# Layer 1's routing without GpSimd, its gather ahead of the overflow's loop, and that loop in a conditional with a branch hint for TensorE

## Chip, cores and metric

One core of one Trainium2 chip runs the whole program in one launch. The metric is device time in microseconds, the median of several executions. All data is float32 in HBM; the 475 MB that the kernel moves are nearly all expert weights.

## What is computed

The reference is a transformer of two layers on 512 tokens of width 1024, conditioned by a vector `c`. Layer 0 mixes tokens by attention, layer 1 by pooling; in each a mixture of 32 experts follows. Cut to what matters here:

```python
for i in range(2):
    sh_m, sc_m, g_m, sh_f, sc_f, g_f = split(silu(c) @ w_ada[i] + b_ada[i], 6)
    x = x + g_m * mixer[i](modulate(rms_norm(x, norm_mix_g[i]), sh_m, sc_m))    # attention, then pooling
    tokens = modulate(rms_norm(x, norm_ffn_g[i]), sh_f, sc_f)
    x = x + g_f * hierarchical_moe(tokens, w_rg[i], w_re[i], w_gu[i], w_down[i])
return rms_norm(x, final_norm_g)

def hierarchical_moe(h, w_rg, w_re, w_gu, w_down):
    gate_g, grp = top_k(softmax(h @ w_rg), 1)              # one of 4 groups
    le = (h @ w_re).reshape(T, 4, 8)[arange(T), grp]       # its 8 experts
    top_v, top_i = top_k(le, 2)                            # the best two
    w_sel = gate_g * softmax(top_v)
    # every token goes to its two experts: (silu(h @ gate) * (h @ up)) @ down, summed with weights w_sel
```

## The kernel before

Instructions stand on each engine in the order in which the code issues them. SyncE's queue streams the weights (class `Stream`, line 118) into a ring of 1 MB tiles; a transfer is issued when a tile comes free, which TensorE's use of an earlier one decides, and `st.fill(n)` says how many may be under way ahead of use.

The stages are: attention (0 to 325 us), its out-projection with layer 0's routing interleaved (`norm_attended`, to 370), the MoE of layer 0 (to 843), the pooling layer with layer 1's routing at its end (`pool_layer` and `route`, to 909), the MoE of layer 1 (to 1387) and the final norm.

Routing of a layer, whose names occur below:

- `norm_high` (L1160, ScalarE) writes a token tile times its norm, rounded, to `xnp`; a second `xnp` holds the low remainder. Layer 0 makes it with `norm_low` (L1164, VectorE, in two halves). Layer 1 goes through `split_norm`: ScalarE makes the same product once more in full (`y`, L1175), and GpSimd subtracts (L1176). There are four token tiles of 128 tokens (`NT`).
- `logits` on TensorE, then `add_shift` (L1186), `choose` (L1222 to L1240: the maxima and their one-hots `r_og`, `r_oh`, then the table `r_M` of tokens and experts), all VectorE.
- `rank` (TensorE L1249, VectorE `r_rk` L1253) counts a token's place within its expert; `fullest_of` (L1260, L1261) counts the fullest expert's tokens, `spread_two` writes `r_oh` for all 32 experts.
- `one_hot` (L1541, VectorE) turns `r_rk` into `OH`, by which TensorE gathers the tokens of a group of four experts (L1014 in layer 0, L1338 elsewhere, 64 matmuls); ScalarE (L1350) and VectorE (L1348) modulate the result to `xe`, in eight tiles.

Each expert has room for `CAP` = 64 tokens. `overflow` stands ahead of each MoE: it copies `r_rk` to `r_tmp` (L1491), every engine loads the fullest expert's count (L1492), and a loop `For_i(CAP, n, CAP)` (L1493) runs the 16 pairs of experts once more for what is over. With these inputs no expert is over 64, so the loop's body is skipped; its code stands between the branch and what follows. In the built program the skip is a compare that falls through, an unconditional branch to the loop's exit, and there a string of semaphore instructions by which all engines wait for each other.

In layer 0 the first group is gathered and modulated ahead of the loop; `moe` gets it as `first`. In layer 1 it is gathered behind it, in `moe`. Then come 16 pairs of experts: `pgate` and `pup` (L1361), `py` (L1386), `pc` (L1415). In the first pair, after 24 of its matmuls, TensorE has the products `pw` (L1321) that sort the tokens' shares into slots; they need `r_rhs` (L1318), the end of VectorE's chain that begins with the one-hots of group 1 and goes over the shares (L1281 to L1297) and `ro` (L1315).

Of the kernel before, what the change touches and what calls it, by code (L numbers as in the profile page):

```python
# [11 lines left out]
F32 = mybir.dt.float32  # L12
F32R = mybir.dt.float32r
# [137 lines left out]
def in_two(z):  # L151

    return z.rearrange("p (q k s) -> p q k s", s=128, k=2)
# [25 lines left out]
class Kernel:  # L179
# [3 lines left out]
    def build(self):  # L183
        tc, nc, a = self.tc, self.nc, self.a
        with ExitStack() as es:
# [12 lines left out]
            with ExitStack() as sm:  # L198
# [7 lines left out]
                norms = self.moe(0, self.prepare_pool(), first=xe, later=later)  # L206
                if self.stop == "moe0":
                    return self.dump_x()
                self.pool_layer(norms)
                if self.stop == "pool":  # L210
                    return self.dump_x()
                self.route()
                self.final(self.moe(1, self.prepare_final(), self.gained))
# [753 lines left out]
    def norm_attended(self):  # L967
# [33 lines left out]
        banks, hl = {}, {}  # L1001
        low = lambda j, k: self.norm_low(j, r[j], *hl[j], k)

        def zeros(k, tag):
            banks[k] = pm.tile([128, 512], F32, tag=tag, name="pga")
            nc.tensor.matmul(banks[k], self.tri_b[:, 0:1].to_broadcast([128, 128]), self.ones_b[:, 0:1].to_broadcast([128, 512]),
                             start=True, stop=False)

        def gather(k, js, parts=range(2)):

            for z in range(2):
                for j in js:
                    for part in parts:
                        nc.tensor.matmul(banks[k][:, z * 256:(z + 1) * 256],  # L1014
                                         self.parts[part][j // 2][:, j % 2, (k + z) * 128:(k + z + 1) * 128], OH[:, j], start=False,
                                         stop=(z == 1 and j == NT - 1 and part == 1))
# [64 lines left out]
        xe = self.big([128, KD, 256], F32, "xe")  # L1081
        for k in range(0, KD, 2):
            gather(k, range(3, 4), (0,))
        for k in range(0, KD, 2):
            gather(k, range(3, 4), (1,))
            for z in range(2):
                self.modulated(0, k + z, banks[k][:, z * 256:(z + 1) * 256], xe[:, k + z])
# [78 lines left out]

    def split_norm(self, j, r, y=None):

        nc = self.nc
        hi, lo = self.norm_high(j, r)  # L1170
        if y is None:
            for k in range(2):
                self.norm_low(j, r, hi, lo, k)
        else:
            nc.scalar.activation(in_two(y), by_two(self.x(j)), AF.Copy, scale=r)  # L1175
            nc.gpsimd.tensor_tensor(lo, y, hi.bitcast(F32), op=ALU.subtract)  # L1176
# [90 lines left out]
    def route(self):  # L1267

        self.route_begin()
        self.choose(slice(0, NT))  # L1270
        self.rank(range(NT))
        self.fullest_of()
        self.spread_two()

# [56 lines left out]
    def gather(self, i, k, OH, n, xe):  # L1331
# [9 lines left out]
        self.modulated(i, k, p[:, :n], xe)  # L1341

# [141 lines left out]
    def overflow(self, i, gf):  # L1484
# [8 lines left out]
        with tc.For_i(CAP, n, CAP):  # L1493
            nc.vector.tensor_scalar(rko, rko, -float(CAP), None, op0=ALU.add)

            whl = self.shares()
            with tc.For_i(0, NPAIR, 1) as p:
                rp = mp.tile([128, NT, 2], F32, name="rp")
                nc.vector.tensor_copy(rp, rko[:, :, ds(2 * p, 2)])
                wp = mp.tile([128, NT, 8], F32R, name="wp")  # L1500
                tw = mp.tile([128, 2, NT, 2], F32, name="tw")
                for z in range(2):
                    for c in range(2):
                        nc.vector.tensor_tensor(tw[:, c], self.oh[c][:, :, ds(2 * p, 2)],
                                                whl[:, z, c].bitcast(F32)[:, :, None].to_broadcast([128, NT, 2]), op=ALU.mult)
                    nc.vector.tensor_tensor(wp[:, :, 2 * z:2 * z + 2], tw[:, 0], tw[:, 1], op=ALU.add)
                nc.vector.tensor_copy(wp[:, :, 4:8], self.tcol[:, :, None].to_broadcast([128, NT, 4]))
                OH = mp.tile([128, NT, 128], F32R, tag="scat", name="OHo", bufs=2)
                for j in range(NT):
                    nc.vector.tensor_tensor(OH[:, j].rearrange("p (e s) -> p e s", e=2),  # L1510
                                            self.iota[:, None, 0:CAP].to_broadcast([128, 2, CAP]),
                                            rp[:, j, :, None].to_broadcast([128, 2, CAP]), op=ALU.is_equal)
                pw = pm.tile([128, 512], F32, tag="t", name="pwo")
                for j in range(NT):
                    nc.tensor.matmul(pw[:, 0:8], OH[:, j], wp[:, j], start=(j == 0), stop=(j == NT - 1))
                s = mp.tile([128, 8], F32, name="so")
                nc.vector.tensor_copy(s, pw[:, 0:8])
                w = mp.tile([128, 1], F32, name="wo")
                for e in range(2):
                    q = slice(64 * e, 64 * e + 64)  # L1520
                    nc.vector.tensor_tensor(w[q], s[q, e:e + 1], s[q, 2 + e:3 + e], op=ALU.add)

                xe = self.fw[:, 1].rearrange("p (k n) -> p k n", k=KD)
                for k in range(KD):
                    self.gather(i, k, OH, 128, xe[:, k])

                def load(name, k):
                    q = slice(k // 2 * 256, (k // 2 + 1) * 256)
                    nc.sync.dma_start(wts, a[name][i, ds(2 * p, 2), q].rearrange("e (p k) n -> p e k n", k=2)[:, :, k % 2])
                    return wts[:, 0], wts[:, 1]  # L1530

                act = self.up(lambda k: xe[:, k], 0, lambda k: load("moe_w_gate_up", k))
                y = self.down(self.turn_act(act), lambda k: load("moe_w_down", k), w, gf)
                P = self.scatter(s[:, 4:5])
                for h in range(2):
                    for unit in self.combine(P, y[h], h):
                        unit()
# [13 lines left out]
    def moe(self, i, late, then=lambda: None, first=None, later=iter(())):  # L1551
# [3 lines left out]
        xe, OH = ({0: first}, {}) if first is not None else ({}, {0: self.one_hot(0)})  # L1555
# [35 lines left out]
        for k in range(KD if first is None else 0):  # L1591
            gather(0, k)
# [61 lines left out]
    def pool_layer(self, norms):  # L1654
# [138 lines left out]
        y = []  # L1793
# [12 lines left out]
        st.fill(RING + 1)  # L1806
        for j in range(1, NT):
            parted(j)
        self.fw = self.gw
        self.row_bcast(self.bank, 5, self.fw[:, 0], nc.scalar)  # L1810

    def row_load(self, name, rows):
# [62 lines left out]
```

## Time and profile before

| | us |
|---|---|
| median of 3 runs | 1399.34 (1399.21 to 1399.42) |
| the profiled execution's own time | 1400.81 |
| its span from first to last instruction | 1398.9 |
| TensorE busy | 1315.8 (94%) |
| VectorE busy | 672.5 (48%) |
| ScalarE busy | 367.7 (26%) |
| GpSimd busy | 153.2 (11%) |
| mean granted TensorE clock | 0.979 of full speed |

All times of rows are microseconds from the span's start in the profiled execution. A busy share is a mean over stages of different kinds; the stages around the change have their own rows below. Branches, semaphore and register instructions are not counted as busy; they are listed on the sequencers (PEldq is TensorE's).

### The profile page before, as it was taken

Reading aid. Unit: us, or ns where it says so; the run is one execution under the profiler, and the core shown is the slowest. Engines: PE = TensorE matmul, PEld = TensorE weight load, DVE = VectorE, ACT = ScalarE, POOL = GpSimd, SP = SyncE. Lnnn points to the kernel's source line nnn. Section 1 sums busy time; section 2 is a strip of 40 time slices with the busy share of each in tenths; the row PEclk is TensorE's granted clock in tenths of the full one; section 3 lists DMA queues with packets and bytes.
Section 4 is the critical chain, followed back from the end, with each engine's and each line's share of the span. In section 5 each row is a group of like instructions: output and inputs, shape, how many; then the busy total and the mean of one; then the engine's idle time right before and its main releaser. Section 6 shows DMA issues by size and latency. Waiting matters only on the chain. (4 is left out here: it accounts for less than half of the span.)

```text
span 1398.9 us, 18564 instructions
## 1 busy us (share of the span) xinstructions
PE 1315.8 (94%) x7134; PEld 737.9 (53%) x7135; DVE 672.5 (48%) x1288; ACT 367.7 (26%) x707; POOL 153.2 (11%) x142
## 2 busy tenths in 40 slices
PE   3799999999899999999999997689999999999995
PEld 1588677778545444454445444554445544454432
DVE  2777788768714343342433437633333433343325
ACT  2454678753211111111111114521111111111103
POOL 1523254430000000000000104200000000000001
PEclk9899999999999999999999998889999999999998
DMA  9412845179489999999999999259999999999993
GB/s 379 155 61 69 353 155 178 52 249 353 182 350 427 426 427 426 427 427 426 427 427 427 420 419 417 98 236 375 426 427 427 426 426 426 427 426 427 426 420 146
DMA packets 80558, 475.45 MB, mean 340 GB/s; under 512 B 8496, under 2 KB 10048, under 8 KB 30288
## 3 DMA queue, kind: packets, MB, share of 16 engines
q1 hardware_dynamic: 80456, 474.19, 82.7%
q8 instruction: 59, 0.97, 0.3%
q14 instruction: 35, 0.29, 0.1%
q10 hardware_dynamic: 8, 0.01, 0.0%
HBM read 472.06 MB, written 2.11 MB: 339 GB/s over the span
## 5 line engine op out<-in xcount | busy, mean ns | idle before, releaser
L1361 PE MATMUL pgate<-wt,xe 128*64 128x512 f32 x1024 | 266.3, 596 | 4.8 <-issue 4.8
L1361 PE MATMUL pup<-wt,xe 128*64 128x512 f32 x1024 | 265.4, 595 | 0.0
L1386 PE MATMUL py<-wt,aT 128*64 128x512 f32 x960 | 212.6, 595 | 0.0
L1366 DVE TENSOR_TENSOR act<-act,pup 128x512 f32<-128x512 f32 x32 | 22.0, 687 | 336.5 <-ACT act L1365 307.0
L1417 DVE TENSOR_TENSOR x<-x,pc 128x512 f32<-128x512 f32 x240 | 153.9, 683 | 32.3 <-PE pc L1415 32.3
L1361 PEld LDWEIGHTS pgate<-wt,xe 128*64 128x64 f32 x1024 | 74.3, 138 | 148.1 <-issue 138.1
L1361 PEld LDWEIGHTS pup<-wt,xe 128*64 128x64 f32 x1024 | 75.0, 138 | 146.5 <-issue 146.4
L1338 PE MATMUL pga<-OH,xnp 128*128 128x256 f32 x960 | 135.2, 286 | 5.5 <-issue 5.5
L1415 PE MATMUL pc<-y,scat 128*128 128x512 f32 x480 | 136.3, 405 | 2.5 <-DVE x L1417 2.5
L1338 PEld LDWEIGHTS pga<-OH,xnp 128*128 128x128 f32 x960 | 128.0, 190 | 14.2 <-issue 7.3
L1399 DVE SCALAR_TENSOR_TENSOR py<-py,r_sw,gw 128x512 f32<-128x512 f32 x64 | 48.5, 758 | 177.5 <-PE py L1386 168.5
L1386 PEld LDWEIGHTS py<-wt,aT 128*64 128x64 f32 x960 | 66.9, 137 | 124.5 <-issue 118.2
L1365 ACT ACTIVATE act<-pgate 128x512 f32<-128x512 f32 x32 | 19.1, 597 | 355.5 <-PE pgate L1361 355.5
L1415 PEld LDWEIGHTS pc<-y,scat 128*128 128x128 f32 x480 | 80.4, 188 | 43.1 <-ACT act L1365 24.3
L1400 ACT ACTIVATE y<-py 128x512 fp32r<-128x512 f32 x64 | 38.2, 596 | 236.7 <-PE py L1386 175.7
L1350 ACT ACTIVATE xe<-pga,mod 128x256 f32<-128x256 f32 x64 | 35.8, 565 | 157.3 <-PE pga L1338 154.2
L545 PE MATMUL pmm<-whl,hT 128*128 128x512 f32 x288 | 69.7, 398 | 0.0
L833 DVE TENSOR_REDUCE mx<-S 128x1 f32<-128x768 f32 x64 | 58.2, 951 | 19.6 <-PE S L830 18.9
L545 PEld LDWEIGHTS pmm<-whl,hT 128*128 128x128 f32 x288 | 54.0, 191 | 11.1
L840 ACT ACTIVATE P<-S,mx 128x768 f32<-128x768 f32 x64 | 57.0, 900 | 2.2 <-POOL rest L714 2.0
L1827 POOL TENSOR_TENSOR xg<-x,gn 128x512 f32<-128x512 f32 x4 | 5.0, 1280 | 479.3 <-DVE x L1449 479.3
L850 PE MATMUL PT<-cst,P 128*128 128x128 f32 x384 | 54.5, 278 | 0.1
(341 smaller groups left out, 1425.8 us busy)
## 6 DMA issues: line engine op xcount, KB each, us to landing
wt<-in_moe_w_gate_up_dram SPq DMA_DIRECT2D x224, 1024.0 KB
wt<-in_moe_w_down_dram SPq DMA_DIRECT2D x120, 1024.0 KB
wt<-in_w_ada_dram SPq DMA_DIRECT2D x48, 1024.0 KB
wt<-in_moe_w_gate_up_dram SPq DMA_DIRECT2D x64, 512.0 KB
wt<-in_moe_w_down_dram SPq DMA_DIRECT2D x16, 512.0 KB
wt<-in_attn_w_qkv_dram SPq DMA_DIRECT2D x6, 1024.0 KB
x<-in_x_dram SPq DMA_DIRECT2D x8, 512.0 KB
wt<-in_attn_w_o_dram SPq DMA_DIRECT2D x4, 1024.0 KB
```

The lines of the kernel that those rows point to most:

```text
L545: self.nc.tensor.matmul(p, lhs(pa, k), whl[pb, k // 4][:, k % 4], start=(k + n == 0), stop=(k == KD - 1 and n == 2))
L833: nc.vector.tensor_reduce(m, s[:, :NKEY], axis=AX, op=ALU.max, negate=True)
L840: nc.scalar.activation(P[n][:, g], S.pop((n, g))[:, :NKEY], AF.Exp, bias=mx[n, g], accum_out=total[n // 4][:, 2 * gp + g, kvl:kvl + 1])
L850: nc.tensor.transpose(pt[:, cc, g * 128:(g + 1) * 128], P[n][:, g, c * 128:(c + 1) * 128], self.ident)
L1338: nc.tensor.matmul(p[:, :n], self.parts[part][j // 2][:, j % 2, k * 128:(k + 1) * 128], OH[:, j], start=(z == 0), stop=(z == 2 * NT - 1))
L1350: nc.scalar.activation(xe, p, AF.Identity, bias=B[:, k:k + 1], scale=A[:, k:k + 1])
L1361: nc.tensor.matmul(p[64 * e:64 * e + 64], xe(k)[:, off + 64 * e:off + 64 * e + 64], w[e][:, h * 512:(h + 1) * 512], start=(k == 0), stop=( ...
L1386: nc.tensor.matmul(py[h][64 * e:64 * e + 64], aT[:, j, 64 * e:64 * e + 64], wd[e][:, h * 512:(h + 1) * 512], start=(j == 0), stop=(j == 3) ...
L1399: nc.vector.scalar_tensor_tensor(py, py, w, gf[:, h * 512:(h + 1) * 512], op0=ALU.mult, op1=ALU.mult)
L1400: nc.scalar.activation(y[:, 0], py, AF.Copy)
L1415: nc.tensor.matmul(p, P[:, j * 128:(j + 1) * 128], y[:, part], start=(part == 0), stop=(part == 1))
L1417: nc.vector.tensor_add(xs, xs, p)
```

## The change

Layer 1's lows are made by `norm_low` on VectorE; `split_norm` and `route` go, and with them GpSimd's four subtractions and ScalarE's four `y`. `pool_layer` now ends with routing and the first group's gather and modulation, written out in order; four matmuls of zeros open the gather's banks. The gather's order is token tiles 0 and 1, then 2, then 3, as the lows become ready. `st.fill` gets one tile less there, so one transfer moves to behind the conditional. The overflow's loop in both layers stands within `tc.If(n > CAP)`, whose skipping arm is the far one, and a hint for TensorE's fetch is marked a little ahead of each.

```diff
@@ pool_layer, from the norm on
-        def parted(j):
-            if j % 2 == 0:
-                y.append(self.big([128, 2, D], F32, "y"))
-            self.split_norm(j, r[:, j:j + 1], y[j // 2][:, j % 2])
-
-        parted(0)
+        def high(j):
+            hl[j] = self.norm_high(j, r[:, j:j + 1])
+
+        def low(j, k):
+            self.norm_low(j, r[:, j:j + 1], *hl[j], k)
+
+        high(0)
         turn(2, "y", nc.vector)
         turn(3, "c", nc.scalar)
+        low(0, 0)
         logits(4, 5, 2, 3)
+        high(1)
+        low(0, 1)
+        low(1, 0)
+        self.route_begin()
         for j in range(NT):
             self.add_shift(j, r[:, j:j + 1])
-        st.fill(RING + 1)
-        for j in range(1, NT):
-            parted(j)
+        st.fill(RING)
+        self.choose(slice(0, NT))
         self.fw = self.gw
         self.row_bcast(self.bank, 5, self.fw[:, 0], nc.scalar)
+        for j in (2, 3):
+            high(j)
+        self.banks = {}
+        for k, tag in ((0, "g"), (2, "u"), (4, "c"), (6, "c")):
+            self.zeros(k, tag)
+        low(1, 1)
+        self.rank(range(NT))
+        OH = mp.tile([128, NT, 256], F32R, name="OH")
+        for j in range(2):
+            self.one_hot_tile(OH, 0, j)
+        self.fullest_of()
+        for j in range(2, NT):
+            self.one_hot_tile(OH, 0, j)
+            for k in range(2):
+                low(j, k)
+        self.spread_two()
+        xe = self.big([128, KD, 256], F32, "xe")
+        for js in (range(2), range(2, 3)):
+            for k in range(0, KD, 2):
+                self.gather_part(OH, k, js)
+        self.tc.mark_branch_hint_location("over1", engines=(mybir.EngineType.PE,))
+        for k in range(0, KD, 2):
+            self.gather_part(OH, k, range(3, 4))
+            for z in range(2):
+                self.modulated(1, k + z, self.banks[k][:, z * 256:(z + 1) * 256], xe[:, k + z])
+        return xe
@@ overflow (the loop's body is the same, indented)
-        with tc.For_i(CAP, n, CAP):
-            nc.vector.tensor_scalar(rko, rko, -float(CAP), None, op0=ALU.add)
+        with tc.If(n > CAP, preferred_fallthrough_block=True, label=f"over{i}"):
+            with tc.For_i(CAP, n, CAP):
+                nc.vector.tensor_scalar(rko, rko, -float(CAP), None, op0=ALU.add)
...
@@ norm_attended, ahead of the gather of token tile 3
+        self.tc.mark_branch_hint_location("over0", engines=(mybir.EngineType.PE,))
@@ moe
-        for k in range(KD if first is None else 0):
-            gather(0, k)
```

The built orders show three places. On TensorE, at layer 1's routing, the gather (`pga`) stood behind the loop's exit; before it came the rank (L1249), the count (L1260) and the loop's compare (L1493), behind which the body's code begins. Before:

```order
L466 MATMUL pb<-gates,cst 128x512 x2
...
L1260 LDWEIGHTS ones_b
L1260 MATMUL pr<-r_M,ones_b 128x32
L1492 TENSOR_LOAD r_fullest
L1493 COMPARE_AND_BRANCH
L1493 UNCONDITIONAL_BRANCH x2
...
L1493 REGISTER_ALU
L1493 COMPARE_AND_BRANCH
L1493 UNCONDITIONAL_BRANCH
L1338 MATMUL pga<-OH,xnp 128x256 x64
L1361 MATMUL pgate<-wt,xe 64x512 x2
```

And now:

```order
L465 MATMUL pb<-gates,cst 128x512 x2
L1315 LDWEIGHTS tri_b
L1315 MATMUL pga<-ones_b,tri_b 128x512
...
L1237 LDWEIGHTS ones_b
L1237 MATMUL pr<-r_M,ones_b 128x32
L1323 MATMUL pga<-OH,xnp 128x256 x64
L1476 TENSOR_LOAD r_fullest
L1477 COMPARE_AND_BRANCH
L1478 COMPARE_AND_BRANCH
L1478 UNCONDITIONAL_BRANCH x2
```

The gather moved ahead of the count's load, behind four matmuls of zeros (L1315); the conditional's compare (L1477) stands ahead of the loop's (L1478).

On VectorE, in the same place, before (L1253 is `r_rk`, L1261 the count, L1240 the spreading, L1541 the one-hots):

```order
L1240 TENSOR_TENSOR r_M<-r_two,r_og 128x128
L1253 SCALAR_TENSOR_TENSOR r_rk<-pr,r_M 128x128
L1261 TENSOR_REDUCE r_fullest<-pr 128x1
L1240 TENSOR_TENSOR r_oh_7180<-r_oh_7176,r_og 128x128
L1240 TENSOR_TENSOR r_oh_7181<-r_oh_7177,r_og 128x128
L1541 TENSOR_TENSOR OH<-cst,r_rk 128x256 x4
L1491 COPY r_tmp<-r_rk 128x128
L1492 TENSOR_LOAD r_fullest
L1493 COMPARE_AND_BRANCH
```

And now, with L1152 the lows, L1526 the one-hots and L1332 VectorE's share of the modulation:

```order
L1217 TENSOR_TENSOR r_M<-r_two,r_og 128x128
L1152 SCALAR_TENSOR_TENSOR xnp<-x,n4r,xnp 128x4x128
L1230 SCALAR_TENSOR_TENSOR r_rk<-pr,r_M 128x128
L1526 TENSOR_TENSOR OH<-cst,r_rk 128x256 x2
L1238 TENSOR_REDUCE r_fullest<-pr 128x1
L1526 TENSOR_TENSOR OH<-cst,r_rk 128x256
L1152 SCALAR_TENSOR_TENSOR xnp<-x,n4r,xnp 128x4x128 x2
L1526 TENSOR_TENSOR OH<-cst,r_rk 128x256
L1152 SCALAR_TENSOR_TENSOR xnp<-x,n4r,xnp 128x4x128 x2
L1217 TENSOR_TENSOR r_oh_7159<-r_oh_7155,r_og 128x128
L1332 TENSOR_SCALAR xe<-pga,mod_7053 128x256 x4
L1477 COMPARE_AND_BRANCH
```

The first two one-hots now follow `r_rk` at once, the lows of token tiles 2 and 3 come between the others, and the modulation stands ahead of the compare; three more lows (L1152) stand ahead of `add_shift` (L1163).

The third place is the hint itself. The code marks it ahead of a few matmuls before the conditional, but the built program has it at the head of the straight stretch of code that the conditional ends: for layer 0 as the second row of TensorE's list, for layer 1 as the first row behind layer 0's conditional.

```order
L1879 UNCONDITIONAL_BRANCH
L1879 BRANCH_PREFETCH_HINT
L333 MATMUL pc<-cst,rowsA 128x96
...
L1478 UNCONDITIONAL_BRANCH
L1477 UNCONDITIONAL_BRANCH
L1879 BRANCH_PREFETCH_HINT
L1345 MATMUL pgate<-wt,xe 64x512 x2
```

Before, those rows had no such hint: the list began with the branch and the same matmul, and behind the loop `pgate` came at once. Counted in instructions, the first hint stands some 1,850 ahead of its branch, the second some 1,900. The other engines have none.

## Rows read from the trace of the kernel before

**Rows 1.** The page: busy time per engine with its share of the span and number of instructions (PE is TensorE, PEld its weight loads), and the shares of the chain that ended last.

```profile
PE 1315.8 (94%) x7134; PEld 737.9 (53%) x7135; DVE 672.5 (48%) x1288; ACT 367.7 (26%) x707; POOL 153.2 (11%) x142
PE 33%; DVE 1%; issue 1%; ACT 0%; DVEq 0%; ACTq 0%
```

**Rows 2.** Busy time by stretch: length, then busy time (and instructions) of PE, PEld, DVE, ACT and POOL, then the granted clock, the share of the DMA engines and GB/s. A steady stretch of the first MoE, and the one that starts with layer 1's gather.

```profile
700.00:729.00 29.00, 29.00 (x150) 14.05 (x148) 11.28 (x20) 3.52 (x6) 0.00 (x0) 1.00 1.01 427
913.00:942.00 29.00, 27.70 (x161) 17.52 (x162) 10.55 (x37) 5.12 (x9) 0.00 (x0) 0.93 0.60 241
```

**Rows 3.** The chain of waits around layer 1's overflow: start, duration, what.

```profile
910.16 3.37 issue
913.53 9.35 PE pga L1338 x64
...
923.44 1.34 DVE OH L1541 x4
...
928.93 0.65 PE pw L1321 x4
```

**Rows 4.** TensorE in order of time around layer 0's overflow: start, duration of the group, line, operation, count, and the idle time before it with what ended it.

```profile
368.18 2.16 PE L1014 MATMUL pga<-OH,xnp 128*128 128x256 f32 x16
375.10 1.97 PE L1361 MATMUL pgate<-wt,xe 128*64 128x512 f32 x4 [4.76 <-issue]
376.86 1.92 PE L1361 MATMUL pup<-wt,xe 128*64 128x512 f32 x4
...
381.50 1.02 PE L1361 MATMUL pgate<-wt,xe 128*64 128x512 f32 x4
382.36 1.02 PE L1361 MATMUL pup<-wt,xe 128*64 128x512 f32 x4
383.31 0.65 PE L1321 MATMUL pw<-r_rhs,ro 128*128 128x96 f32 x4
```

**Rows 5.** The loop's line, by engine and kind, in 366 to 377 (the first two) and in 906 to 915 (the last): count, shortest, median and longest in ns, first and last start.

```profile
L1493 PEldq EVENT_SEMAPHORE  x9: 51/51/51, 370.4 to 374.7; - x9
L1493 PEldq COMPARE_BRANCH  x3: 100/193/3345, 369.1 to 374.9; - x3
...
L1493 PEldq COMPARE_BRANCH  x3: 82/187/3252, 908.8 to 913.3; - x3
```

**Rows 6.** The queues that carry instructions: packets, MB, share of 16 engines, in 366 to 376, and q8, TensorE's, over the whole span.

```profile
q14 instruction: 2, 0.02, 1.1%
q8 instruction: 1, 0.02, 0.6%
...
q8 instruction: 59, 0.97, 0.3%
```

**Rows 7.** Busy time by stretch, columns as in rows 2: layer 0's routing, its first MoE products up to `pw`, and layer 1's gather.

```profile
330.00:375.00 45.00, 39.28 (x259) 33.32 (x258) 33.87 (x125) 15.88 (x29) 0.00 (x0) 0.99 0.56 222
375.10:383.30 8.20, 8.20 (x24) 2.27 (x24) 5.78 (x21) 0.42 (x2) 1.26 (x1) 0.64 0.94 367
913.50:922.90 9.40, 9.37 (x66) 9.24 (x68) 1.63 (x4) 2.26 (x4) 0.00 (x0) 0.82 0.14 57
```

**Rows 8.** ScalarE (the first) and VectorE in order of time around layer 0's overflow, columns as in rows 4.

```profile
369.67 1.93 ACT L1350 ACTIVATE xe<-pga,mod 128x256 f32<-128x256 f32 x4 [0.76 <-PE pga L1014]
...
370.27 1.91 DVE L1348 TENSOR_SCALAR xe<-pga,mod 128x256 f32<-128x256 f32 x4 [1.70 <-ACT xe L1350]
372.10 0.22 DVE L1491 COPY r_tmp<-r_rk 128x128 f32<-128x128 f32 x1
374.28 1.43 DVE L1541 TENSOR_TENSOR OH<-cst,r_rk 128x256 fp32r<-128x256 f32 x4 [1.97 <-issue]
...
379.32 0.48 DVE L1318 TENSOR_TENSOR r_rhs<-r_oh,r_whl 128x128 fp32r<-128x128 f32 x2
```

**Rows 9.** GpSimd (the first) and VectorE in order of time in layer 1's routing, columns as in rows 4.

```profile
895.10 7.00 POOL L1176 TENSOR_TENSOR xnp<-y,xnp 128x1024 fp32r<-128x1024 f32 x3 [0.71 <-ACT y L1175]
...
895.72 0.74 DVE L1186 SCALAR_TENSOR_TENSOR L<-pb,n4r,bw 128x36 f32<-128x36 f32 x4 [3.32 <-PE pb L1742]
896.71 5.54 DVE L1213 SCALAR_TENSOR_TENSOR r_og<-L,r_m,cst 128x4 f32<-128x4 f32 x4
...
903.65 0.64 DVE L1213 SCALAR_TENSOR_TENSOR r_oh<-r_le,r_v,cst 128x8 f32<-128x8 f32 x4
```

**Rows 10.** Layer 0's routing, by line and form, columns as in rows 5: VectorE's `r_og` and one pair of lows.

```profile
L1213 DVE SCALAR_TENSOR_TENSOR r_og<-L,r_m,cst x2: 221/222/224, 353.8 to 362.7; 128x4 f32<-128x4 f32 x2
L1164 DVE SCALAR_TENSOR_TENSOR xnp<-x,n10r,xnp x2: 741/742/743, 342.0 to 343.5; 128x512 fp32r<-128x512 f32 x2
```

**Rows 11.** TensorE (the first), VectorE and ScalarE (the last two) in order of time from layer 1's rank to its gather's end, columns as in rows 4.

```profile
906.91 0.19 PE L1249 MATMUL pr<-r_M,tri_b 128*128 128x32 bf16 x1 [9.50 <-DVE r_M L1240]
...
906.56 0.29 DVE L1240 TENSOR_TENSOR r_M<-r_two,r_og 128x128 bf16<-128x128 f32 x1
907.37 0.29 DVE L1253 SCALAR_TENSOR_TENSOR r_rk<-pr,r_M 128x128 f32<-128x128 f32 x1 [0.52 <-PE pr L1249]
...
920.06 0.56 ACT L1350 ACTIVATE xe<-pga,mod 128x256 f32<-128x256 f32 x1 [1.33 <-PE pga L1338]
921.95 0.56 ACT L1350 ACTIVATE xe<-pga,mod 128x256 f32<-128x256 f32 x1 [1.33 <-PE pga L1338]
```

**Rows 12.** Weights: a stretch of the first MoE, columns as in rows 2; GB/s in 40 slices of 1370 to 1380; and TensorE's last products of layer 1's experts, columns as in rows 4.

```profile
400.00:405.00 5.00, 5.00 (x28) 1.59 (x24) 0.22 (x1) 0.00 (x0) 0.00 (x0) 1.00 0.40 110
...
GB/s 270 238 229 229 229 238 238 246 172 74 41 33 8 0 0 0 0 0 0 0 0 0 0 0 0 0 0 0 0 0 0 0 0 0 0 0 0 0 0 0
...
1381.12 1.94 PE L1434 MATMUL py<-wt,aT 128*64 128x512 f32 x8
```

More of the change, by code (lines that the diff above doesn't have):

```diff
@@ L205, in build @@
                     return self.dump_x()
-                norms = self.moe(0, self.prepare_pool(), first=xe, later=later)
+                norms = self.moe(0, self.prepare_pool(), xe, later=later)
                 if self.stop == "moe0":
                     return self.dump_x()
-                self.pool_layer(norms)
+                xe = self.pool_layer(norms)
                 if self.stop == "pool":
                     return self.dump_x()
-                self.route()
-                self.final(self.moe(1, self.prepare_final(), self.gained))
+                self.final(self.moe(1, self.prepare_final(), xe, self.gained))
     def dump_x(self):
@@ L1000, in norm_attended @@
         OH = mp.tile([128, NT, 256], F32R, name="OH")
-        banks, hl = {}, {}
+        self.banks, hl = {}, {}
         low = lambda j, k: self.norm_low(j, r[j], *hl[j], k)
[L1004 to L1016, printed above, removed]
+        zeros = self.zeros
+        gather = lambda k, js, parts=range(2): self.gather_part(OH, k, js, parts)
         def product(j, ks, p):
@@ L1086, in norm_attended @@
             for z in range(2):
-                self.modulated(0, k + z, banks[k][:, z * 256:(z + 1) * 256], xe[:, k + z])
+                self.modulated(0, k + z, self.banks[k][:, z * 256:(z + 1) * 256], xe[:, k + z])
         def later():
@@ L1165, in norm_low @@
                                             op0=ALU.mult, op1=ALU.subtract)
[L1167 to L1176, printed above, removed]
     def logits(self, j, h, t):
@@ L1265, in spread_two @@
             self.spread(self.oh[c], self.oh8[c], slice(0, NT))
[L1267 to L1273, printed above, removed]
     def shares(self):
@@ L1341, in gather, with zeros, gather_part @@
         self.modulated(i, k, p[:, :n], xe)
+    def zeros(self, k, tag):
+        p = self.banks[k] = self.pm.tile([128, 512], F32, tag=tag, name="pga")
+        self.nc.tensor.matmul(p, self.tri_b[:, 0:1].to_broadcast([128, 128]), self.ones_b[:, 0:1].to_broadcast([128, 512]), start=True,
+                              stop=False)
+    def gather_part(self, OH, k, js, parts=range(2)):
+        for z in range(2):
+            for j in js:
+                for part in parts:
+                    self.nc.tensor.matmul(self.banks[k][:, z * 256:(z + 1) * 256],
+                                          self.parts[part][j // 2][:, j % 2, (k + z) * 128:(k + z + 1) * 128], OH[:, j], start=False,
+                                          stop=(z == 1 and j == NT - 1 and part == 1))
     def modulated(self, i, k, p, xe):
@@ L1492, in overflow @@
         n = nc.values_load(self.fullest[0:1, 0:1], min_val=0, max_val=SEQ, skip_runtime_bounds_check_because="a count of tokens")
-        with tc.For_i(CAP, n, CAP):
-            nc.vector.tensor_scalar(rko, rko, -float(CAP), None, op0=ALU.add)
[L1496 to L1537, printed above, removed]
@@ L1549, in one_hot, with moe @@
         return OH
-    def moe(self, i, late, then=lambda: None, first=None, later=iter(())):
+    def moe(self, i, late, first, then=lambda: None, later=iter(())):
         nc, st = self.nc, self.st
         gf = self.fw[:, 0]
-        xe, OH = ({0: first}, {}) if first is not None else ({}, {0: self.one_hot(0)})
+        xe, OH = {0: first}, {}
         def gather(g, k):
```

42 lines of the change are left out of this document (41 added, 1 removed).

## The prediction

> **What bounds the kernel now.** I read the page first: TensorE is busy 94% of the span, and the chain that ended last runs through its MoE products [rows 1]. By stages, a steady stretch of the first MoE keeps TensorE busy in all of its 29.00 us at full clock, with the DMA engines full as well, while the stretch after layer 1's routing has 1.3 us of idle time and a clock of 0.93 [rows 2]. So the change can only count in the two seams between routing and MoE. The chain of waits names the second: 3.37 us of "issue" that no work explains, the gather of 9.35 us, one-hots and the chain of the shares up to the first `pw` at 928.93 [rows 3]. Both MoE phases have their length whatever comes ahead, so I measure each seam by when the first `pw` starts: 383.31 in layer 0, 928.93 in layer 1.
>
> **Seam of layer 0.** TensorE's last gather ends at 370.34. Then nothing runs until 375.10 [rows 4]. The sequencer's rows on the loop's line say why: of its three branches one takes 3345 ns, and the exit behind it is a string of 51 ns semaphore instructions, nine in all [rows 5]. In the same window one packet of TensorE's instruction queue lands [rows 6]: the branch past the loop's body waits for code. After the gap the clock is low: groups of four `pgate` or `pup` matmuls start 1.7 us apart at first and 0.86 apart later, and the stretch up to the first `pw` has a mean granted clock of 0.64 [rows 4, 7].
>
> The change replaces compare, unconditional branch and eight-fold exit by one compare whose taken arm is hinted to TensorE. If the hint works, a branch costs what the short ones in the same rows do, 0.1 to 0.2 us [rows 5]. The first product then waits for what it really needs: ScalarE's last modulated tile, ended at 371.60, and ScalarE's pass through the arm behind it, some 0.1 [rows 8]. So `pgate` starts near 371.7, 3.4 earlier. An idle stretch of 1.4 us need not drop the clock: between 330 and 375 TensorE idles 5.7 us in short pieces at 0.99 [rows 7]. If so, the 24 matmuls ahead of the first `pw` take 5.2 us (six groups of 0.86) and end at 376.9. But what is late next is VectorE: its one-hot starts at 374.28 after its own exit events; it ended its last modulate at 372.18 and its copy at 372.32 [rows 8]. With load, branch and one event it should start at 372.9 to 373.2, and from one-hot to a ready `r_rhs` is 5.5 us here (374.28 to 379.80 [rows 8]). So the first `pw` starts near 378.6: **4.7 us** earlier.
>
> Bounds of this term: 5.2 if VectorE's exit shrinks to 0.3; 2.2 if the code still has to be fetched. In that case the fetch starts at the compare, 369.2, ahead of the last matmuls, instead of at 370.53, and 0.9 of exit events goes: `pgate` 2.2 earlier, at about 372.9, a gap of 2.6 and again a low clock at 3.0 lost, so the first `pw` at 381.1.
>
> **Seam of layer 1.** Removed: four ScalarE copies of 1.24 and four GpSimd subtractions. Their own time lies beside other work. Their harm is in VectorE's rows: four `r_og` of 128x4 elements take 5.54 us, from 896.71 to 902.25, as GpSimd's last three subtractions run until 902.10, while four `r_oh`, twice as wide, take 0.64 [rows 9]; layer 0's `r_og`, with GpSimd idle, take 0.22 each [rows 10]. So `choose` ends 5.54 - 0.64 = **4.9 us** earlier; `r_M` is ready at 901.96. Added on VectorE: eight `norm_low` of 0.74 [rows 10]. Three stand ahead of the logits, where VectorE idled 3.32 us [rows 9], one in the wait for the rank's 0.52 us (some 0.1 over), and four after the one-hots 0 and 1. They cost nothing so long as TensorE is still in the 32 matmuls of tokens 0 and 1: those take at least 3.8 us, and VectorE is done with all in about 4. Added on TensorE: four zero matmuls in idle time, the 9.5 us before the rank [rows 11].
>
> Moved: the 64 gather matmuls from behind the conditional to ahead of it, with the one-hots before `r_fullest`. Before, from `r_M` ready (906.85) the rank's answer `r_rk` starts at 907.37 and takes 0.29, then `r_fullest`, `r_oh`, one-hots, load, branch and fetch follow until 913.53 [rows 11, 3]. Now the gather follows two one-hots of 0.36: 901.96 + 0.52 + 0.10 + 0.29 + 0.7 = about 903.5, **10 us earlier**. It lasts 9.33 as before if the clock stays as poor at first (mean 0.82 [rows 7]), 7.55 at full clock (16 matmuls per 1.89 us [rows 11]), and perhaps 11 if the clock stays low longer, since TensorE idles from 897.4 but for the zeros [rows 11]. I take 9.3, the row nearest: it ends at 912.8 instead of 922.86. Then VectorE modulates its last tile (0.54), copies 0.22, loads and branches (some 0.8 as in layer 0), and its one-hot of group 1 starts 1.6 us after the gather, where it was 0.5 [rows 3]. That wait is new: the queue behind it is the whole chain of shares. From one-hot to `pw` is 5.57 [rows 3], so `pw` starts at 920.0: **8.9 us** earlier. TensorE's branch costs nothing here: its 24 matmuls end at 918.8 with a hint and at about 920.3 without. Bounds: 10.5 with a gather at full clock, 7 with one of 11 us.
>
> SyncE's one weight transfer that moves from ahead of the conditional to behind it finds time: in layer 0's MoE, 25 us after that seam, the DMA engines are down to a share of 0.40 [rows 12]. Its queue is released by TensorE's use of tiles, so transfers shift with it. The last weights land at 1373 while the last `py` starts at 1381 [rows 12], 8 us of cover; if the transfers did not shift at all, all but about 1 us of layer 1's gain would still stand.
>
> **Sum.** 4.7 + 8.9 = 13.6 off a profiled span of 1398.9, which gives 1385.3. The profiled run took 1400.81, 1.47 over the median of 1399.34; taking the same 13.6 off the median gives **1385.7 us**.
>
> **Rivals.**
> 1. *The hint saves nothing.* No row of this kernel shows a hint at work, and the built order speaks for it: the hint stands first on TensorE's list, some 1,850 instructions before its branch, and the second some 1,900 before its own. Gain: 2.2 in layer 0; in layer 1 8.6, as `pw` waits 0.3 for TensorE. Together 10.8: 1388.5. Chance 0.25. A rule speaks for it too: the Trainium skill, "Runtime: NRT & Kernel Launch", section "Instruction fetch mechanics", says that prefetch is purely sequential and that a taken branch outside the current window of two blocks of code forces a fetch before execution goes on. By this rule the time would be this rival's; the fetch of before agrees with it, and whether a hint is an exception no run here shows yet.
> 2. *Clock and VectorE take more.* A low clock at the start of both seams, unhinted branches of ScalarE or VectorE that have to fetch too (two packets of the other instruction queue land in layer 0's window [rows 6]), and a gather of 11 us: 3 + 6 = 9 or less, 1390.5. Chance 0.13.
> 3. *The conditional gives nothing and GpSimd was not the cause*, say because VectorE's lows now delay `choose` as GpSimd did: eight lows are 5.9 us, 1 more than the 4.9 of excess now. Then layer 0 gains nothing, and in layer 1 the gather starts 10 - 4.9 - 1 = 4.1 earlier and ends at 918.8; with 3.3 of branch and 0.9 of exit behind it `pgate` starts at 923.0, where it starts now: no change, 1399. Against it: three lows have an idle place, and four stand behind the first one-hots. Chance 0.04.
> 4. *Slower: the hint spoils the sequential fetch.* It runs far too early, at the head of the block; if it makes the fetcher drop code that is needed in between, TensorE would stall there at up to the 3.3 us that a fetch costs here [rows 5]. Its 14,269 matmuls and weight loads came in 59 packets [rows 1, 6], 242 to a packet, so the two hinted stretches of some 1,850 and 1,900 instructions are about 15 packets. Four such stalls eat the 13.6 us; all of them would give 1399.3 - 13.6 + 15 x 3.3 = about 1435. From the fifth on it is slower. Chance 0.04; nothing in the trace shows it, and nothing excludes it.
>
> **How the numbers follow.** The forecast has 0.54, with 1382.5 to 1387.5 of its own (gains of 12 to 16.8: both seams at their better bounds make 15.7). Rival 1 lies at 1387.5 to 1389.5 and rival 2 up to 1392. The range 1382.5 to 1391.5 holds the forecast, rival 1 and most of rival 2, less tails: about 0.82. A change of 0.2% (2.8 us) is what a measurement here can tell from none. Faster: forecast, rivals 1 and 2 and some of the tails, 0.92; same 0.04; slower 0.04.
>
> **What would show it.** Right: no branch over 0.3 us on TensorE's sequencer at the conditionals; `pgate` of layer 0 within 0.3 of 371.7 at full clock; its `pw` released by VectorE; four `r_og` in 0.9 us; the gather beginning near 903.5 and ending near 912.8; `pw` near 920 by the old clock, less what layer 0 gained. Wrong: a branch of 2 to 3 us that stays (rival 1), a fetch gap in the middle of a MoE (rival 4), TensorE waiting for weights late in either MoE.

## The result, and the profile after

| | before | changed |
|---|---|---|
| median, us | 1399.42 (1399.21 to 1402.32) | 1391.02 (1387.70 to 1391.12) |
| ratio of the runs | | 0.9926, interval 0.9914 to 0.9938 |
| the same on another chip | 1400.16 (1398.54 to 1402.98) | 1388.36 (1387.09 to 1389.98) |
| ratio there | | 0.9916, interval 0.9903 to 0.9929 |

The change makes the kernel 8.4 us faster by the first medians, about 10.4 by the first ratio and 11.8 by the second. Forecast were 13.6 us, 1385.7. The profiled execution of the changed kernel took 1391.02, with a span of 1388.9. Cut at the points by which the prediction measures, the two profiles compare so:

| stretch, us | before | changed | difference | forecast |
|---|---|---|---|---|
| start to the end of layer 0's first gather | 370.34 | 371.92 | +1.58 | 0 |
| to the first `pw` | 12.97 | 8.54 | -4.43 | -4.7 |
| to the second `pw` | 2.44 | 3.00 | +0.56 | 0 |
| to layer 1's norm (`n4r` done) | 503.73 | 503.82 | +0.09 | 0 |
| to the first `pw` of layer 1 | 39.45 | 31.18 | -8.27 | -8.9 |
| to the end | 469.92 | 470.44 | +0.52 | 0 |

The norm, from which layer 1's seam is measured, is done at 889.48 before and at 887.28 in the changed kernel (start, duration):

```profile
889.32 0.16 DVE L498 TENSOR_TENSOR n4r<-n4r,n4t 128x4 f32<-128x4 f32 x1
...
887.12 0.16 DVE L497 TENSOR_TENSOR n4r<-n4r,n4t 128x4 f32<-128x4 f32 x1
```

Both seams did what was forecast, to within 0.7 us. TensorE in order of time at layer 0's overflow, changed kernel (start, duration, count, idle time before and what ended it):

```profile
369.76 2.15 PE L1323 MATMUL pga<-OH,xnp 128*128 128x256 f32 x16
373.27 1.08 PE L1345 MATMUL pgate<-wt,xe 128*64 128x512 f32 x4 [1.35 <-ACTq L1477]
374.70 1.08 PE L1345 MATMUL pup<-wt,xe 128*64 128x512 f32 x4 [0.35 <-DVEq L1477]
...
380.46 0.65 PE L1290 MATMUL pw<-r_rhs,ro 128*128 128x96 f32 x4 [1.25 <-DVE r_rhs L1287]
...
383.46 0.65 PE L1290 MATMUL pw<-r_rhs,ro 128*128 128x96 f32 x4 [0.48 <-DVE r_rhs L1287]
```

Against [rows 4] the gap of 4.76 is 1.35, ended by ScalarE's event as expected; behind one more wait, 0.35 for VectorE's event, the groups are 0.86 to 0.91 apart, and the first `pw` waits for VectorE. TensorE's branch, in layers 0 and 1, on the conditional's line (shortest, median, longest in ns), against 3345 and 3252 in [rows 5]:

```profile
L1477 PEldq COMPARE_BRANCH  x1: 384/384/384, 370.6 to 370.6; - x1
...
L1477 PEldq COMPARE_BRANCH  x1: 350/350/350, 909.2 to 909.2; - x1
```

The two hints stand in the same trace at 0.8 and 372.1 us, 370 and 537 us ahead of these branches:

```profile
L1879 PEldq BRANCH_PREFETCH_HINT  x2: 31/40/50, 0.8 to 372.1; - x2
```

Layer 1's routing and gather, VectorE and TensorE in order of time, same columns:

```profile
894.51 0.62 DVE L1190 SCALAR_TENSOR_TENSOR r_og<-L,r_m,cst 128x4 f32<-128x4 f32 x4
899.45 0.29 DVE L1217 TENSOR_TENSOR r_M<-r_two,r_og 128x128 bf16<-128x128 f32 x1
...
901.12 9.92 PE L1323 MATMUL pga<-OH,xnp 128*128 128x256 f32 x64 [0.19 <-DVE OH L1526]
911.87 1.08 PE L1345 MATMUL pgate<-wt,xe 128*64 128x512 f32 x4 [0.82 <-ACTq L1477]
912.74 1.43 DVE L1526 TENSOR_TENSOR OH<-cst,r_rk 128x256 fp32r<-128x256 f32 x4 [0.38 <-DVEq L1477]
...
918.46 0.65 PE L1290 MATMUL pw<-r_rhs,ro 128*128 128x96 f32 x4 [1.23 <-DVE r_rhs L1287]
```

The four `r_og` take 0.62 for 5.54 [rows 9]. From the norm (887.28 here, 889.48 before) `r_M` is ready after 12.46 us instead of 17.38, and the gather starts after 13.84 instead of 24.05. It lasts 9.92 instead of 9.33, and VectorE's one-hot stands 1.70 behind its end. By stretch (columns as in [rows 2]), the first products run at full clock, where [rows 7] had 0.64; the gather's clock fell to 0.76 from 0.82:

```profile
373.30:380.40 7.10, 5.56 (x24) 1.51 (x24) 5.29 (x23) 1.68 (x3) 0.00 (x0) 1.00 0.62 242
901.10:911.00 9.90, 9.88 (x64) 9.72 (x64) 4.87 (x12) 1.34 (x3) 0.00 (x0) 0.76 0.01 2
```

The second `pw` of layer 0 is late by the mechanism that the change took out of layer 1. VectorE's last two `r_rhs` there take 1.56 us, the same two 0.49 in the first round, and GpSimd runs at the same time:

```profile
379.92 0.49 DVE L1287 TENSOR_TENSOR r_rhs<-r_oh,r_whl 128x128 fp32r<-128x128 f32 x2
...
381.84 1.56 DVE L1287 TENSOR_TENSOR r_rhs<-r_oh,r_whl 128x128 fp32r<-128x128 f32 x2
381.93 1.32 POOL L436 TENSOR_TENSOR gates<-gates,ada_rows 64x512 f32<-64x512 f32 x1 [67.17 <-DMA wt<-in_moe_w_gate_up_dram]
```

The other profiles with a conditional bear this out. In e5, e8, e9 and e10 `gates` began beside the first of these two operations, they took 1.55 to 1.56, and the second `pw` came 2.99 to 3.00 behind the first, as here. In e1, e2, e4, e6 and e7 `gates` began after both had begun, in e11 it had ended; they took 0.48 to 0.49, and it came 2.44 to 2.45 behind.

### The profile page after: what moved, and what is told of

It is laid out like the page before. It is cut to its first block, busy times and chain, and to the rows that moved or that the text cites. A ratio compares the mean times of both kernels' runs of the same rounds, so it can differ in the third digit from the quotient of the medians.

```text
span 1388.9 us, 18512 instructions
## 1 busy us (share of the span) xinstructions
PE 1318.5 (95%) x7137; PEld 738.9 (53%) x7139; DVE 674.4 (49%) x1296; ACT 362.8 (26%) x703; POOL 143.9 (10%) x138
## 5 line engine op out<-in xcount | busy, mean ns | idle before, releaser
L1307 PE MATMUL pga<-OH,xnp 128*128 128x256 f32 x896 | 125.9, 283 | 0.0
L1307 PEld LDWEIGHTS pga<-OH,xnp 128*128 128x128 f32 x896 | 118.9, 188 | 8.5 <-issue 1.6
```

Source lines behind the costliest of these rows:

```text
L1307: nc.tensor.matmul(p[:, :n], self.parts[part][j // 2][:, j % 2, k * 128:(k + 1) * 128], OH[:, j], start=(z == 0), stop=(z == 2 * NT - 1))
```

## The experiments

My theory at this point: the two seams gain some 12 us and repeat, VectorE's chain bounds both, and what is missing to the forecast lies where the change does nothing. The seams of every profile, in us; "last pair" is from the first `py` of layer 0's fifteenth pair to the last `py` of its sixteenth:

| kernel | median (ratio) | gather's end to `pgate`, layer 0 | to `pw` | norm to `pw`, layer 1 | last pair, layer 0 |
|---|---|---|---|---|---|
| before | | 4.76 | 12.97 | 39.45 | 35.93 |
| changed | 1391.02 (0.9926) | 1.35 | 8.54 | 31.18 | 36.44 |
| e1 no hint | 1388.35 (0.9915) | 2.69 | 8.53 | 30.44 | 36.52 |
| e2 conditional only | 1392.65 (0.9948) | 1.36 | 8.54 | 36.19 | 36.05 |
| e3 routing only | 1396.28 (0.9970) | 4.91 | 13.17 | 35.36 | 38.73 |
| e4 three hints | 1389.70 (0.9922) | 1.36 | 8.65 | 31.18 | 39.18 |
| e5 changed again | 1388.36 (0.9916) | 1.36 | 8.54 | 30.64 | 38.18 |
| e6 GpSimd busy | 1395.60 (0.9964) | 1.36 | 8.54 | 35.72 | 38.39 |
| e7 late one-hots | 1387.54 (0.9908) | 1.36 | 7.28 | 29.30 | 36.28 |
| e8 more zeros | 1389.77 (0.9921) | 1.36 | 8.54 | 30.78 | 36.27 |
| e9 pad in layer 0 | 1390.24 (0.9919) | 1.36 | 8.54 | 30.56 | 35.30 |
| e10 pad in layer 1 | 1393.05 (0.9934) | 1.36 | 8.54 | 30.71 | 38.53 |
| e11 late one-hots, no hint | 1388.25 (0.9899) | 2.49 | 9.49 | 30.76 | 36.19 |

e1 to e4 ran on one chip, e5 to e8 on a second, e9 to e11 on a third. Intervals of the ratios are 0.0012 to 0.0019 either way, so kernels 1.5 us apart are told apart by their seams, not by their medians.

**e1, the change without its hints.** Edit, and the same for `over1`:

```diff
-        self.tc.mark_branch_hint_location("over0", engines=(mybir.EngineType.PE,))
```

> The change without its two hints. Theory A (VectorE's chain to the first pw bounds both seams, so the hint buys nothing visible): the branch past the loop takes about 3.3 us again, but it is issued 1.3 and 1.9 us before the gathers end, so pgate starts about 0.8 us later in both seams, still ends its 24 matmuls before r_rhs is ready, and the time is that of the change within 0.5 us, if the clock does not fall in the longer gap. Rival B (the hint carries the gain): 2 to 3 us slower than the change. Rival C (the hint at the head of the program costs the 1.6 us by which attention was longer): 1.6 us faster than the change.

TensorE's branch on the conditional's line, and what follows:

```profile
L1476 PEldq COMPARE_BRANCH  x1: 3562/3562/3562, 370.1 to 370.1; - x1
...
374.11 1.08 PE L1344 MATMUL pgate<-wt,xe 128*64 128x512 f32 x4 [2.69 <-PEq L1476]
374.99 1.06 PE L1344 MATMUL pup<-wt,xe 128*64 128x512 f32 x4
...
379.95 0.65 PE L1289 MATMUL pw<-r_rhs,ro 128*128 128x96 f32 x4 [0.47 <-DVE r_rhs L1286]
```

The branch takes 3.56 us and `pgate` comes 1.33 later, but `pw` still waits for VectorE and starts 8.53 after the gather, as with the hint. The hint works (384 against 3562 ns, from the head of the program), and in this kernel it bought nothing: theory A. The medians agree, 1388.35 here and 1388.36 for the changed kernel in e5, though on two chips. The delay of `pgate` was larger than the 0.8 expected, and theory A's condition, that the clock does not fall in the longer gap, held in this profile; in e11 it fell in a shorter one.

The conditional alone is what shortens the seam: its compare is issued 1.3 us ahead of the gather's end, and one 51 ns event follows instead of the exit's string. Of the 4.44 gained against before, 2.07 is `pgate`'s earlier start and 2.37 the clock: the 24 products and the wait behind them take 5.84 at full clock, where they took 8.21 at 0.64. Attention gives no support to C: layer 0's gather ended at 369.9 to 372.7 in nine profiles with a hint ahead of it and at 370.2 to 371.4 in four without; a cost below 1 us is not excluded.

**e2, the conditional alone, and e3, the routing alone.** Edits: to before (e2) and, from the change, the other way round (e3):

```diff
# e2: in before's overflow; in route the mark "over1" ahead of spread_two, in norm_attended "over0"
+        with tc.If(n > CAP, preferred_fallthrough_block=True, label=f"over{i}"):
+            with tc.For_i(CAP, n, CAP):
# e3: in the change's overflow; no marks
-        with tc.If(n > CAP, preferred_fallthrough_block=True, label=f"over{i}"):
-            with tc.For_i(CAP, n, CAP):
+        with tc.For_i(CAP, n, CAP):
```

> The kernel before with the conditional and its hints alone; layer 1's routing and the gather behind the conditional as before. Theory A: layer 0 gains what it gained in the change (4.4 us from the gather's end to the first pw, 0.5 of it given back at the second pw); in layer 1 the gather starts some 4.3 us earlier than 24.05 us after the norm, and the time is 7 to 8 us under before. Rival (the moved gather and the routing without GpSimd carry most of it): 4 us or less under before.

> The change without conditional and hints: layer 1's new routing and its gather ahead of the bare loop. Theory A: the gather ends as in the change, 9.6 us earlier than before, but the exit of the loop now stands between it and pgate as in layer 0 before (4.8 us), with a low clock behind it at 3 us more: first pw of layer 1 gains 2.7 to 5.6 us, and layer 0 nothing. Rival (the gather's move is the gain and the exit hides behind it): 8 us or more under before.

e2 gained 4.43 in layer 0 and 3.26 in layer 1, e3 nothing in layer 0 and 4.09 in layer 1, as theory A has them, but for the 0.5 that e2 was to give back at the second `pw`: it came 2.44 behind the first, as before, since `gates` began later there. In e3 the old exit keeps `pgate` 4.67 behind the gather. Layer 1's two parts add up to 7.35 where together they gain 8.27 to 8.8: the exit is a wait that e2 takes away and e3 keeps, and behind it e3's products begin at a low clock (granted 0.5 from 921.1 to 924.5). That this clock is what keeps the parts from adding up is argued, not shown.

**e4, hints for VectorE and ScalarE.** Edit, in both marks:

```diff
-engines=(mybir.EngineType.PE,)
+engines=(mybir.EngineType.PE, mybir.EngineType.DVE, mybir.EngineType.Activation)
```

> The change with the hints for VectorE and ScalarE too. In the change VectorE's branch and its event stood 0.6 us apart and ScalarE's 0.5, with no work between. Theory A (VectorE bounds the first pw, and its branch fetches): both one-hots start 0.4 us earlier and the time is 0.8 us under the change. Rival (those gaps are no fetch, or something else bounds pw): no difference.

A miss: `pw` came 8.65 after the gather in layer 0 and 31.18 after the norm in layer 1. The hints were there, on VectorE at 0.8 and 372.8 us and on ScalarE at 0.7 and 371.3, and in layer 0 the events stood 0.6 and 0.5 us behind their branches as without them. So the gap between those engines' branch and event is not a fetch that a hint saves.

**e5, the change again, and e6, GpSimd busy.** Edit of e6, ahead of `add_shift`:

```diff
+        y = self.big([128, 2, D], F32, "y")
+        for j in range(3):
+            nc.gpsimd.tensor_tensor(y[:, 0], self.x(j), hl[1][0].bitcast(F32), op=ALU.subtract)
```

> The changed kernel once more, on the same chip as the three below, since its first runs spread from 1387.7 to 1391.1 us and the kernel without hints gave 1388.4 elsewhere. Theory (the seams gain 12.1 us, and what else differs between runs lies where the change does nothing: attention, the end of layer 0's MoE, the pooling layer): the seams repeat within 0.2 us (8.5 us from the gather's end to the first pw in layer 0, 31.2 us from the norm to the first pw in layer 1), while attention or the stretch from the second pw to layer 1's norm differ by over 1 us from the first profile. Rival (the seams vary): one of the two is off by more than 0.5 us.

> The change with three GpSimd subtractions of 128x1024 put back beside choose in layer 1; their result goes nowhere. Theory (they block VectorE): choose's r_og take about 5 us again, r_M is ready 4 to 5 us later, and the time is 4 to 5 us over the change. Rival (GpSimd was harmless, and choose was held up by its data): no difference.

e5's seam of layer 0 is the same to 0.01; layer 1's is 0.54 shorter, 0.56 of it in the gather (9.36 for 9.92: the low clock lay 3.4 us over it, and 4.7 in the first profile). So the rival is right by 0.04 on the number; what varies is the clock at the gather. Attention was 1.8 shorter than in the first profile, the last pair 1.7 longer. In e6, in order of time:

```profile
894.36 7.72 POOL L1795 TENSOR_TENSOR y<-x,xnp 128x1024 f32<-128x1024 f32 x3 [23.06 <-ACT xnp L1148]
...
897.04 2.76 DVE L1190 SCALAR_TENSOR_TENSOR r_og<-L,r_m,cst 128x4 f32<-128x4 f32 x4
...
900.04 2.07 DVE L1196 TENSOR_TENSOR r_og<-r_og,r_best 128x16 f32<-128x16 f32 x1
```

The four `r_og` take 2.76 for 0.62, and a small operation behind them 2.07 for 0.17; `r_M` is ready 16.49 after the norm, 4.03 later. GpSimd did block VectorE. Of the price of 4.9 this shows 4.03, spread over two operations, where the expectation had all of it in `r_og`. The median is 7.2 over e5, more than the 4 to 5 expected; the two profiles are 9.7 apart, 4.0 of it in the routing, 1.1 in the gather, and the rest in stages without the edit.

**e7, group 1's one-hots behind the shares.** Edit:

```diff
-        early = self.slots()
+        early = self.slots(lambda: OH.update({1: self.one_hot(1)}))    # called ahead of r_sl
...
-            if p % 2 == 0 and p + 2 < NPAIR:
+            if p % 2 == 0 and 0 < p < NPAIR - 2:
                 OH[g + 1] = self.one_hot(g + 1)
```

> The change with group 1's one-hots (1.43 us of VectorE) moved from ahead of the chain of shares to behind it, in both layers. Theory (VectorE's chain to the first pw bounds both seams): pw starts 1.6 us earlier in layer 0 (6.9 after the gather's end instead of 8.5) and 1.4 earlier in layer 1 (6.0 instead of 7.4); layer 1's part reaches the end, layer 0's only as far as the weights of its last pair are there, so 1.4 to 3.0 us under the change. Rival (something else releases pw): no difference.

VectorE was the bound: `pw` comes 7.28 after the gather in layer 0 (1.26 earlier) and 6.30 in layer 1 instead of 7.42, now without a wait:

```profile
378.40 1.03 PE L1346 MATMUL pup<-wt,xe 128*64 128x512 f32 x4
379.40 0.65 PE L1290 MATMUL pw<-r_rhs,ro 128*128 128x96 f32 x4
```

The expectation had it 1.6 and 1.4 earlier: with VectorE out of the way TensorE's own products are the bound. Its median is 0.8 under e5's, less than the 1.4 to 3.0 expected, and the intervals do not tell the two apart. By its seams it is the version I would keep.

**e8, more matmuls of zeros ahead of the rank.** Edit, after the four `zeros`, which it adds to:

```diff
+        for _ in range(14):
+            nc.tensor.matmul(self.banks[0], self.tri_b[:, 0:1].to_broadcast([128, 128]),
+                             self.ones_b[:, 0:1].to_broadcast([128, 512]), start=False, stop=False)
```

> The change with 14 more matmuls of zeros on TensorE ahead of layer 1's rank, in what was 3.7 us of idle time. Theory (the idle time lowers the clock at the gather's start): the granted clock stays at 1.00 through the gather, which takes 7.6 to 8.0 us instead of 9.9, and the time is 2 us under the change. Rival (the gather waits for VectorE's lows and one-hots): it takes over 9 us at full clock, and no gain.

A miss of both. TensorE was busy for 5.94 of the 6.60 us ahead of the rank instead of 2.96 in e5, and the clock fell all the same, at the gather's start, 0.60 in its first 4.2 us; it took 9.52:

```profile
892.50:899.10 6.60, 5.94 (x26) 2.58 (x25) 5.71 (x31) 3.38 (x4) 0.00 (x0) 1.00 0.00 0
899.10:900.40 1.30, 0.63 (x14) 0.45 (x14) 1.26 (x4) 0.00 (x0) 0.00 (x0) 1.00 0.00 0
900.40:904.60 4.20, 4.20 (x21) 4.10 (x22) 4.11 (x10) 0.00 (x0) 0.00 (x0) 0.60 0.00 2
```

**e9 and e10, a pad of 3.2 us in either MoE.** The table's last column has a spread of 3 us in code that no edit touches. Edit, at the head of the loop over pairs, with 0 or 1 for the layer:

```diff
+            if (i, p) == (0, 9):
+                pad = self.pm.tile([128, 512], F32, tag="t", name="pad")
+                for z in range(14):
+                    nc.tensor.matmul(pad, ..., start=(z == 0), stop=(z == 13))
```

> The change with 14 idle matmuls of zeros (3.2 us of TensorE) ahead of the tenth pair of layer 0's MoE. Theory (the weights of that MoE's last pair set its end: in seven profiles of kernels that share this part the last pair's stretch took 0.1 to 3.3 us over its 35.93): the pad gives the weights time, the stretch from the eighth pair of py's to the last py loses what it was over 35.9 besides the pad's own 3.2 or less, and the time rises by under 3.2 us, by 1 to 2.7 against the change's 1388.4. Rival (the last pair's overtime is another thing, such as the clock): the overtime stays and the time rises by all of 3.2.

> The same pad ahead of the tenth pair of layer 1's MoE, as the control: there the weights had 8 us of cover in the profile of before. Theory: the time rises by the pad's whole 3.2 us. Rival (weights set the end there too): it rises by less.

TensorE's weight loads for `pgate` from 780 to 845 (busy time, mean ns, then idle time before them by what ended it), first with the pad in layer 0, then with the pad in layer 1:

```profile
L1345 PEld LDWEIGHTS pgate<-wt,xe 128*64 128x64 f32 x64 | 5.1, 137 | 8.7 <-issue 7.9 <-PE py L1370 0.5 <-DMA wt<-in_moe_w_gate_up_dram 0.3
```

```profile
L1345 PEld LDWEIGHTS pgate<-wt,xe 128*64 128x64 f32 x56 | 4.8, 136 | 10.4 <-issue 5.8 <-DMA wt<-in_moe_w_gate_up_dram 4.3 <-PE py L1370 0.3
```

With the pad in layer 0 the last pair takes 35.30, the least of all profiles; without it, on the same chip, 38.53 with seven waits for weights. From the second `pw` to the last `py` of layer 0 the two took 455.15 and 455.14: against that profile the pad, which made its own pair 3.33 longer, cost layer 0 nothing. Against other profiles of the same code it cost something, 0.4 against e5 (454.78) and 2.2 to 2.3 against the first profile and e8 (452.93 and 452.88), whose last pairs had less to wait. In layer 1 it cost its whole length: from the first `pw` to the end 473.80 in e10, 470.45 in e9. The medians differ by 2.81. So layer 0's MoE ends when its weights are there, with a stall that differs from run to run, and layer 1's does not. Before was at that limit too: its last pair took 0.63 over the least, e3's 3.43.

**e11, e7 without hints.** Edit: those of e1 and e7 together.

> The kernel with group 1's one-hots behind the shares, without the two hints. Theory (with VectorE out of the way TensorE's own branch bounds the first pw): pgate starts 1.3 us later in layer 0 and 1.1 later in layer 1 than with hints (2.7 and 1.9 after the gathers' ends instead of 1.36 and 0.83), pw about 0.9 later each (8.2 after the gather's end instead of 7.3 in layer 0). Rival (the hint is worth nothing here either): pw within 0.2 us of 7.28 after the gather's end in layer 0.

With VectorE out of the way the branch counts: `pgate` is 2.49 behind the gather instead of 1.36, in layer 1 2.40 instead of 0.83, and `pw` 2.2 and 1.4 later than in e7, more than the 0.9 expected. In layer 0 a low clock follows the longer gap, with groups 1.28 and 1.71 apart instead of 0.86:

```profile
372.64 1.08 PE L1345 MATMUL pgate<-wt,xe 128*64 128x512 f32 x4 [2.49 <-PEq L1477]
373.52 1.55 PE L1345 MATMUL pup<-wt,xe 128*64 128x512 f32 x4
374.80 1.98 PE L1345 MATMUL pgate<-wt,xe 128*64 128x512 f32 x4
376.51 1.49 PE L1345 MATMUL pup<-wt,xe 128*64 128x512 f32 x4
```

The medians of e7 and e11 stand on two chips and their ratios overlap, so the hint's worth is shown in the seams and not in the time.

## Why the prediction was right, and where it was off

The sign and the mechanism of both seams held. The time lies in the range (1382.5 to 1391.5), but partly by luck: 1391.02 is above the forecast's own band, which ended at 1387.5, and inside only because the range was widened for the rivals. It is nearest to rival 2's 1390.5, and the second chip's 1388.36 to rival 1's 1388.5; as the items below show, neither rival's mechanism is what happened. Two of the prediction's own signs went against it: the branches took 384 and 350 ns, where none over 0.3 us was to be left, and weight loads waited 1.4 us for weights late in layer 0's MoE (0.7 before).

- *Layer 0's seam*: `pgate` came where it was put (forecast 1.36 after the gather, measured 1.35), at full clock, and `pw` was VectorE's. 4.43 for 4.7. Unforeseen was 0.56 at the second `pw`, from GpSimd's `gates` beside `r_rhs`.
- *Layer 1's seam*: `choose` gained 4.92 for 4.9, the gather's start 10.2 for 10; VectorE's one-hot stood 1.70 behind the gather for 1.6. The term that was mis-sized is the gather: 9.92 where I took "9.3, the row nearest", because the low clock lay over more of it. 8.27 for 8.9.
- *Rival 1*, that the hint saves nothing, was priced at 2.8 us of the sum, on the ground that the late branch brings a low clock and TensorE behind VectorE. In e1 the branch was as late as said (2.69 for 2.6), the clock stayed, and VectorE covered it: 0. In e11 the clock fell in nearly the same gap. In e1 a packet of TensorE's instruction queue started 1.0 us into the branch of 3.56 and landed within it. The rule that I cited from the Trainium skill, "Runtime: NRT & Kernel Launch", "Instruction fetch mechanics", that a taken branch out of the window forces a fetch, agrees with that; the hinted branch of 384 ns is an exception to it.
- *Rival 2*, a low clock in both seams, fetches of ScalarE and VectorE, and a gather of 11 us, showed only in part of the gather's term (9.92). Layer 0's first products ran at full clock, and e4's hints for those engines changed nothing.
- *Rival 3* fell by `choose` here and by e6, and its conditional that gives nothing by e2.
- *Rival 4*, that the hint spoils other fetches, did not show: the stretches to layer 1's norm and to the end grew by 0.09 and 0.52, and TensorE's queue brought 57 packets, 59 in e1 without hints. Its price was worked out with two counts that do not go together. The 1,850 and 1,900 are rows of the built program, where a product stands as one; 242 to a packet counts weight loads too. The trace has 16 and 21 packets between hint and branch, 37 for its 15.
- *The sum* is the step that was off: "taking the same 13.6 off the median". The profiled run of before was 1.4 over its median in this result (1399.42), that of the changed kernel was its median, and between the two profiles stages without any edit differ by 2.19 (attention 1.58, the end 0.52, the middle 0.09). With the seams' 0.27 + 0.56 + 0.63 that is 5.1 of the 5.2 us that separate 13.6 from the medians' 8.4. Attention's part goes with the clock: its mean from 20 to 60 us was 0.83 before, 0.70 in the first profile of the change and 0.79 in e5, where attention was 0.2 shorter than before. Over all thirteen profiles layer 0's gather ended at 369.9 to 370.3 where that clock was 0.83 and at 371.9 to 372.7 where it was 0.70. That the low clock makes attention longer is argued from these rows; I tried no edit on it. The middle's 0.09 hides two parts, 0.51 more in the last pair and 0.41 less in the pooling layer, which from layer 0's last `py` to the norm took 49.2 in five profiles and 50.7 to 51.3 in the other eight.
- *The weights*: I looked for cover at the end of layer 1 only, where e10 agrees that there is some. At the end of layer 0 there was none. The seam's gain there still reached the end on the whole, as transfers shift with TensorE's use of tiles, but the stall varies by 3 us from run to run. By the packets, what landed from 420 to 800 came at 0.4057 MB/us (MB of 1024 KB) in the change's first profile and at 0.4043 in e5, which over those 380 us is 1.3 us of its 1.7 of longer last pair. That does not explain the others: in e4, with the longest last pair (39.18), it was 0.4055. Why the stall varies stays open.

Open is how much of the 8.4 to 11.8 is chip and run: the seams and the second `pw` make 12.1 in the first profile, 12.7 in e5.

## What to carry to other kernels

Cost a change by the stretch between two fixed points, not by the span: layer 0's seam repeated here to 0.1 us and layer 1's to 0.6, where whole runs spread over 3. Ask what bounds the engine after the stall is gone; here a VectorE chain two steps away made a hint that works worth nothing in the seam until that chain was moved. And look for cover at the end of every stage that a saving must pass: a pad of known length shows whether a stage is paced by TensorE or by its weights, where the stretch without it has been seen in more than one profile.

## What I had not expected of the hardware

- A hint far ahead of its branch still works: 370 and 537 us and 16 and 21 packets of instructions ahead, 384 and 350 ns where the unhinted branch took 3562.
- 14 more matmuls, which fill TensorE's idle time ahead of the rank, did not keep its clock up (e8): 0.60 in the gather's first 4.2 us.
- One GpSimd operation of 1.3 us lengthens a VectorE operation beside it by about 1.1 (0.49 to 1.56 for two `r_rhs`). In e3 it went the other way: VectorE's `ro` had begun 0.09 us before `gates` and took its usual 0.69, and `gates` took 1.72 instead of 1.26.
